# RMSNorm with each row written twice: one 32 KB store run per partition, one DMA queue, fused multiply

## The chip, the cores and the metric

The kernel runs on one core of one Trainium2 chip. The metric is device microseconds (us) per execution, as the median of several runs; lower is better. Single runs that were over 1.5% above the fastest of the same kernel are called slow and are left out of the ratios.

## The reference

```python
x: (8, 512, 2048) float32, gamma: (2048,) float32
x_rep = np.repeat(x, 2, axis=1)                       # every row twice, next to each other
rms = np.sqrt((x_rep ** 2).mean(axis=-1, keepdims=True) + 1e-6)
return x_rep / rms * gamma                            # (8, 1024, 2048) float32
```

At least 33.56 MB must be read from HBM and 67.11 MB written to it.

## The kernel before

A tile is 128 partitions x 2 rows x 2048 elements (16 KB per partition, 2 MB); there are 16 tiles. Loads go out on SP's hardware DMA queue, stores on GpSimd's software queue, two stores per tile, one for each copy of the rows.

```python
K = 2
x_t   = x_f.rearrange("(n p k) d -> n p k d", p=P, k=K)
out_t = out_v.rearrange("(n p k) r d -> n p k r d", p=P, k=K)
BUFS = 6                                   # 6 input tiles, 6 work/output tiles
# ... gamma is loaded first, on SP, and broadcast to all partitions by GpSimd ...
for i in range(ntiles):
    x_tile = xin.tile([P, K, D], f32)
    nc.sync.dma_start(out=x_tile[:], in_=x_t[i])
    sq_tile = sq.tile([P, K, D], f32)
    for k in range(K):                     # ACT: squares and their sum
        nc.scalar.activation(out=sq_tile[:, k, :], in_=x_tile[:, k, :], func=Square,
                             accum_out=ss[:, k : k + 1])
    # ... ACT: rms = sqrt(ss / D + eps); DVE: rstd = 1 / rms ...
    y_tile = sq_tile                       # the squares' tile is used again for the output
    for k in range(K):
        nc.vector.tensor_scalar_mul(out=y_tile[:, k, :], in0=x_tile[:, k, :], scalar1=rstd[:, k : k + 1])
    nc.vector.tensor_mul(out=y_tile[:], in0=y_tile[:], in1=gamma_kd)
    for r in range(R):                     # two stores; HBM runs of one row, 8 KB
        nc.gpsimd.dma_start(out=out_t[i, :, :, r, :], in_=y_tile[:])
# ... (cut)
```

## Time and profile before

| | before |
|---|---|
| time, median | 245.0 us |
| span of the profiled run | 243.0 us |
| DVE / ACT busy | 46% / 29% |
| HBM read, written | 33.56 MB, 67.11 MB |

The page of the kernel before, its utilisation rows (40 equal slices of the span of 6.1 us; a digit is the busy share in tenths, the last row is GB/s of all 16 DMA engines) and its DMA queues (packets, MB, share of the time of 16 engines):

```profile
DVE  0069999950900049680095709577595600000000
...
DMA  6999999999999999999999999999999999999993
GB/s 222 431 431 431 391 433 429 436 417 442 422 431 430 433 422 431 429 427 430 425 430 450 410 426 426 430 425 430 429 425 418 418 417 419 430 417 425 417 426 160
...
q0 software_dynamic: 8704, 67.11, 65.7%
q1 hardware_dynamic: 2306, 33.56, 32.8%
```

The DMA row is full from the second slice to the last but one. No engine comes near it, so the time is the time that the DMA engines need. The costliest groups of instructions (line, engine, operation, operands, count; then busy us, mean ns of one; then the engine's idle time before them and who ended it):

```profile
L64 ACT ACTIVATE sq_tile<-x_tile 128x2048 f32<-128x2048 f32 x32 | 60.8, 1901 | 114.1 <-DMA out_dram<-sq_tile 101.1
L87 DVE TENSOR_TENSOR sq_tile<-sq_tile,gamma_b 128x4096 f32<-128x4096 f32 x16 | 70.8, 4422 | 0.5
...
L84 DVE TENSOR_SCALAR sq_tile<-x_tile,rstd 128x2048 f32<-128x2048 f32 x32 | 40.2, 1298 | 0.5
```

ACT's 101 us of waiting for a store to leave is a buffer coming free late: a sign of the DMA bound, not a cost. The trace also has a record of every DMA packet. A load is 2048 packets of 16 KB, nearly all of 611 ns; the stores are 8192 packets of 8 KB, nearly all of 309 ns.

### The profile page before, as it was taken

The page shows a single profiled execution, that of the slowest core. Times are in us where ns is not written, and L with a number is a line of the kernel's source. Part 1 is how long each engine was busy: PE and PEld are TensorE (multiplying, and loading weights), DVE is VectorE, ACT ScalarE, POOL GpSimd, SP SyncE. Part 2 cuts the span into 40 slices and gives each one's busy share as a digit, 9 for nine tenths or more (in the row PEclk, how much of TensorE's full clock was granted, in tenths as well). Part 3 has the DMA queues.
Part 4 walks back from the last instruction along what each step waited for, and adds up shares of the span by engine and source line. Part 5 has one row for each costly group of instructions (what it writes and reads, how often), then busy time and mean ns, then how long its engine had stood idle before and what let it go on. Part 6 is the DMA issues. An engine that isn't in the chain of part 4 may idle for free.

```text
span 243.0 us, 320 instructions
## 1 busy us (share of the span) xinstructions
DVE 112.7 (46%) x65; ACT 69.5 (29%) x82; POOL 30.2 (12%) x37
## 2 busy tenths in 40 slices
DVE  0069999950900049680095709577595600000000
ACT  2598656006000150600615061541624000000000
POOL 4003223411010101110130111111121111000000
DMA  6999999999999999999999999999999999999993
GB/s 222 431 431 431 391 433 429 436 417 442 422 431 430 433 422 431 429 427 430 425 430 450 410 426 426 430 425 430 429 425 418 418 417 419 430 417 425 417 426 160
DMA packets 11012, 100.69 MB, mean 414 GB/s; under 512 B 769, under 2 KB 769, under 8 KB 769
## 3 DMA queue, kind: packets, MB, share of 16 engines
q0 software_dynamic: 8704, 67.11, 65.7%
q1 hardware_dynamic: 2306, 33.56, 32.8%
q14 instruction: 2, 0.02, 0.0%
HBM read 33.56 MB, written 67.11 MB: 414 GB/s over the span
## 4 chain that ended last, share of the span: by engine, by line
DMA 50%; another core or an unknown queue 15%; issue 4%; ACT 3%; DVE 2%; POOL 1%; POOLq 0%; ACTq 0%
DMA out_dram<-sq_tile 50%; ACT sq_tile L64 3%; DVE sq_tile L87 2%; POOL out_dram L90 1%; POOLq L116 0%; ACT rms L72 0%; DVE rstd L80 0%; ACTq L64 0%; POOLq L90 0%
## 5 line engine op out<-in xcount | busy, mean ns | idle before, releaser
L64 ACT ACTIVATE sq_tile<-x_tile 128x2048 f32<-128x2048 f32 x32 | 60.8, 1901 | 114.1 <-DMA out_dram<-sq_tile 101.1
L87 DVE TENSOR_TENSOR sq_tile<-sq_tile,gamma_b 128x4096 f32<-128x4096 f32 x16 | 70.8, 4422 | 0.5
L90 POOL DMA_DIRECT2D out_dram<-sq_tile x32 | 27.7, 867 | 169.3 <-DMA out_dram<-sq_tile 125.6
L84 DVE TENSOR_SCALAR sq_tile<-x_tile,rstd 128x2048 f32<-128x2048 f32 x32 | 40.2, 1298 | 0.5
L80 DVE RECIPROCAL rstd<-rms 128x2 f32<-128x2 f32 x16 | 2.6, 163 | 77.8 <-ACT rms L72 77.8
L64 ACT ACTIVATION_READ_ACCUMULATOR sq_tile<-x_tile 128x1 f32 x32 | 6.0, 186 | 0.0
L72 ACT ACTIVATE rms<-ss,eps_t 128x2 f32<-128x2 f32 x16 | 4.7, 296 | 0.5
L45 POOL PARTITION_BROADCAST gamma_b<-gamma_b x1 | 2.3, 2293 | 2.1 <-DMA gamma_b<-in_gamma_dram 2.1
L64 ACT ACT_TABLE_LOAD x1 | 1.3, 1283 | 0.7 <-PEq L105 0.7
L72 ACT ACT_TABLE_LOAD x1 | 1.3, 1283 | 0.0
L53 DVE MEMSET eps_t<- 128x1 f32 x1 | 0.1, 59 | 0.8 <-PEq L105 0.8
L105 POOL MEMSET const-float32-0.0<- 128x1 f32 x1 | 0.1, 99 | 0.2 <-issue 0.2
L105 POOL MEMSET const-uint8-127<- 128x1 uint8 x1 | 0.1, 103 | 0.0
L105 POOL MEMSET const-bfloat16-1.0<- 128x1 bf16 x1 | 0.1, 102 | 0.0
L105 POOL MEMSET const-float32-1.0<- 128x1 f32 x1 | 0.1, 99 | 0.0
## 6 DMA issues: line engine op xcount, KB each, us to landing
out_dram<-sq_tile POOLq DMA_DIRECT2D x32, 2048.0 KB, 40.7
x_tile<-in_x_dram SPq DMA_DIRECT2D x16, 2048.0 KB, 24.4
gamma_b<-in_gamma_dram SPq DMA_DIRECT2D x1, 8.0 KB
```

The costliest lines, as they stand in the source:

```text
L45: nc.gpsimd.partition_broadcast(out_ap=gamma_b[:], in_ap=gamma_b[0:1, :])
L53: nc.vector.memset(eps_t, eps)
L64: nc.scalar.activation(out=sq_tile[:, k, :], in_=x_tile[:, k, :], func=mybir.ActivationFunctionType.Square, accum_out=ss[:, k : k + 1],)
L72: nc.scalar.activation(out=rms[:], in_=ss[:], func=mybir.ActivationFunctionType.Sqrt, scale=inv_d, bias=eps_t[:],)
L80: nc.vector.reciprocal(out=rstd[:], in_=rms[:])
L84: nc.vector.tensor_scalar_mul(out=y_tile[:, k, :], in0=x_tile[:, k, :], scalar1=rstd[:, k : k + 1])
L87: nc.vector.tensor_mul(out=y_tile[:], in0=y_tile[:], in1=gamma_kd)
L90: nc.gpsimd.dma_start(out=out_t[i, :, :, r, :], in_=y_tile[:])
L105: nc = _bacc.Bacc("TRN2", target_bir_lowering=False, num_devices=1)
```

## The change

The intent: fewer and longer DMA runs. The output buffer holds both copies of a row, so a tile goes out as one DMA with one 32 KB run per partition, on SP's hardware queue behind the loads. DVE multiplies by the reciprocal and by gamma in one pass and copies the result; the squares go to PSUM, where nobody reads them. There are five input and three output buffers, and the first load is issued before gamma's.

```diff
-    BUFS = 6
-    xin = ctx.enter_context(tc.tile_pool(name="xin", bufs=BUFS))
-    sq = ctx.enter_context(tc.tile_pool(name="sq", bufs=BUFS))
+    AHEAD = 5
+    xin = ctx.enter_context(tc.tile_pool(name="xin", bufs=AHEAD))
+    yout = ctx.enter_context(tc.tile_pool(name="yout", bufs=3))
+    junk = ctx.enter_context(tc.tile_pool(name="junk", bufs=1, space=bass.MemoryType.PSUM))
 ...
+    out_t = out.rearrange("b s d -> (b s) d").rearrange("(n p j) d -> n p (j d)", p=P, j=K * R)
+    load(0)
+    # ... gamma, now on ACT's queue; then load(1) to load(AHEAD - 1)
     for i in range(ntiles):
-        y_tile = sq_tile
+        y = yout.tile([P, K, R, D], f32, name="y")
 ...
         for k in range(K):
-            nc.vector.tensor_scalar_mul(
-                out=y_tile[:, k, :], in0=x_tile[:, k, :], scalar1=rstd[:, k : k + 1]
-            )
-        nc.vector.tensor_mul(out=y_tile[:], in0=y_tile[:], in1=gamma_kd)
-        for r in range(R):
-            nc.gpsimd.dma_start(out=out_t[i, :, :, r, :], in_=y_tile[:])
+            nc.vector.scalar_tensor_tensor(
+                out=y[:, k, 0, :], in0=xt[:, k, :], scalar=rstd[:, k : k + 1], in1=gamma_b[:],
+                op0=Alu.mult, op1=Alu.mult,
+            )
+            nc.vector.tensor_copy(out=y[:, k, 1, :], in_=y[:, k, 0, :])
+        nc.sync.dma_start(out=out_t[i], in_=y.rearrange("p k r d -> p (k r d)"))
+        if i + AHEAD < ntiles:
+            load(i + AHEAD)
```

(Cut: the squares, square root and reciprocal, which only change buffers.)

More of the change, by code (lines that the diff above doesn't have):

```diff
@@ L19 @@
     P = nc.NUM_PARTITIONS
+    f32 = mybir.dt.float32
+    Act = mybir.ActivationFunctionType
+    Alu = mybir.AluOpType
     B, S, D = x.shape
@@ L23 @@
     R = So // S
-    assert D == Do and B == Bo and So == S * R
+    assert R == 2 and D == Do and B == Bo and So == S * R
     eps = 1e-6
-    x_f = x.rearrange("b s d -> (b s) d")
+    inv_d = 1.0 / float(D)
+    K = 2
     N = B * S
-    K = 2
     assert N % (P * K) == 0
     ntiles = N // (P * K)
-    x_t = x_f.rearrange("(n p k) d -> n p k d", p=P, k=K)
-    out_v = out.rearrange("b (s r) d -> (b s) r d", r=R)
-    out_t = out_v.rearrange("(n p k) r d -> n p k r d", p=P, k=K)
-    BUFS = 6
+    x_t = x.rearrange("b s d -> (b s) d").rearrange("(n p k) d -> n p k d", p=P, k=K)
@@ L41, with load @@
     small = ctx.enter_context(tc.tile_pool(name="small", bufs=8))
-    gamma_b = singles.tile([P, D], mybir.dt.float32)
-    nc.sync.dma_start(out=gamma_b[0:1, :], in_=gamma.partition_broadcast(1))
-    nc.gpsimd.partition_broadcast(out_ap=gamma_b[:], in_ap=gamma_b[0:1, :])
-    gamma_kd = bass.AP(
-        tensor=gamma_b.tensor,
-        offset=gamma_b.offset,
-        ap=[gamma_b.ap[0], [0, K], gamma_b.ap[1]],
-    )
-    eps_t = singles.tile([P, 1], mybir.dt.float32)
+    xs = []
+    def load(i):
+        xt = xin.tile([P, K, D], f32, name="xt")
+        nc.sync.dma_start(out=xt[:], in_=x_t[i])
+        xs.append(xt)
@@ L53 @@
+    load(0)
+    gamma_b = singles.tile([P, D], f32, name="gamma_b")
+    nc.scalar.dma_start(out=gamma_b[0:1, :], in_=gamma.partition_broadcast(1))
+    nc.gpsimd.partition_broadcast(out_ap=gamma_b[:], in_ap=gamma_b[0:1, :])
+    eps_t = singles.tile([P, 1], f32, name="eps_t")
     nc.vector.memset(eps_t, eps)
-    inv_d = 1.0 / float(D)
+    for i in range(1, AHEAD):
+        load(i)
     for i in range(ntiles):
-        x_tile = xin.tile([P, K, D], mybir.dt.float32, name="x_tile")
-        nc.sync.dma_start(out=x_tile[:], in_=x_t[i])
-        sq_tile = sq.tile([P, K, D], mybir.dt.float32, name="sq_tile")
-        ss = small.tile([P, K], mybir.dt.float32, name="ss")
+        xt = xs[i]
+        y = yout.tile([P, K, R, D], f32, name="y")
+        ss = small.tile([P, K], f32, name="ss")
@@ L63 @@
         for k in range(K):
-            nc.scalar.activation(
-                out=sq_tile[:, k, :],
-                in_=x_tile[:, k, :],
-                func=mybir.ActivationFunctionType.Square,
-                accum_out=ss[:, k : k + 1],
-            )
-        rms = small.tile([P, K], mybir.dt.float32, name="rms")
-        nc.scalar.activation(
-            out=rms[:],
-            in_=ss[:],
-            func=mybir.ActivationFunctionType.Sqrt,
-            scale=inv_d,
-            bias=eps_t[:],
-        )
@@ L79 @@
-        rstd = small.tile([P, K], mybir.dt.float32, name="rstd")
-        nc.vector.reciprocal(out=rstd[:], in_=rms[:])
-        y_tile = sq_tile
-        for k in range(K):
-            nc.vector.tensor_scalar_mul(
-                out=y_tile[:, k, :], in0=x_tile[:, k, :], scalar1=rstd[:, k : k + 1]
-            )
-        nc.vector.tensor_mul(out=y_tile[:], in0=y_tile[:], in1=gamma_kd)
-        for r in range(R):
-            nc.gpsimd.dma_start(out=out_t[i, :, :, r, :], in_=y_tile[:])
+            sq = junk.tile([P, D], f32, name="sq")
@@ new lines @@
+            nc.scalar.activation(out=sq[:], in_=xt[:, k, :], func=Act.Square, accum_out=ss[:, k : k + 1])
+        rms = small.tile([P, K], f32, name="rms")
+        nc.scalar.activation(out=rms[:], in_=ss[:], func=Act.Sqrt, scale=inv_d, bias=eps_t[:])
+        rstd = small.tile([P, K], f32, name="rstd")
+        nc.vector.reciprocal(out=rstd[:], in_=rms[:])
+        for k in range(K):
+            nc.vector.scalar_tensor_tensor(
+                out=y[:, k, 0, :], in0=xt[:, k, :], scalar=rstd[:, k : k + 1], in1=gamma_b[:],
+                op0=Alu.mult, op1=Alu.mult,
+            )
+            nc.vector.tensor_copy(out=y[:, k, 1, :], in_=y[:, k, 0, :])
```

## The prediction

> **What bounds it now.** The DMA engines. The utilisation rows show their share at 9 tenths or more in 38 of 40 slices, 414 GB/s mean over the span and about 430 in the middle; DVE is busy 46%. HBM traffic is 33.56 MB read and 67.11 MB written, unchanged. The waits view agrees: ACT waits 101 us and POOL 126 us for stores.
>
> **Packet cost.** In the trace's packet records a load is 2048 packets of 16 KB, nearly all 611 ns; a store is 8192 packets of 8 KB, nearly all 309 ns. Two sizes give an estimate: 302 ns per 8 KB plus about 7 ns per packet. At the floor, loads cost 2048 x 611 / 16 = 78.2 us and stores 8192 x 309 / 16 = 158.2 us, together 236.4 of the 237.7 us between the first and the last data packet. The rest of the 243.0 us span is 2.1 us before the first packet and about 3 us after the last. About 1 us is store packets of 312 to 319 ns; about 1 us is slow first packets of the load stream; and about 0.6 us (estimate) is the dip to 395 GB/s at 24 to 30 us, where load packets stretch as the first store starts. The Trainium skill ("DMA: Bandwidth & Descriptors", section "Bandwidth") gives a 435 GB/s fabric ceiling; these durations give 429 (16 KB) and 424 (8 KB).
>
> **What the change does.**
> - Stores become one 32 KB run per partition on SP's hardware queue. If one packet carries it: 4 x 302 + 7 = 1215 ns (estimate) against 4 x 309 = 1236, which saves 2.7 us over 2048 runs on 16 engines; if cut at 16 KB, 1222 ns and 1.8 us saved. [...]
> - The first load is issued before gamma: about 0.4 us earlier.
> - The software queue goes, perhaps with the dip and slow late packets: 0 to 1.5 us.
> - DVE: the two scale passes and the 4.42 us multiply per tile (7.05 us with the reciprocal) become two fused multiplies (estimate 2.2 us each, half of 4.42) and two copies (estimate 1.3, as the scale pass): about 7.2 us per tile. Hidden under 14.6 us of DMA per tile.
> - Squares go to PSUM: no effect.
> - Three output buffers and one in-order queue of store i, load i+5. A store's buffer comes free, DVE needs 7 us, and two other stores and three loads (about 34 us, estimate) are still queued: the queue should not run dry. The first store is ready near 21.6 us, before the five loads end.
>
> All the gain is DMA packet time, on the critical path; the DVE changes are off it.
>
> **Prediction.** Span: 1.7 to the first packet + 78.2 + 155.5 to 156.4 + about 2 of slow packets + 2.7 = about 240.4 us; plus the 2.0 us by which the time exceeds the span: 242.4 us. Range 240.0 to 244.6. Faster by over 2% (under 240.1): 0.11; within 2%: 0.86; slower: 0.03.
>
> **What would show it.** Store packets of 32 KB near 1215 ns (or 16 KB near 611); no software queue; DMA share 9 everywhere; no dip; mean near 419 GB/s.
>
> **What would make it wrong.** Slow packets vanish entirely or run packets exceed my line: under 240. In-order queueing leaves gaps, or 32 KB stores run at more ns per byte: over 245.

## The result, and the profile after

The changed kernel takes 244.01 us (243.73 to 244.77, four runs) against 245.0 us. The ratio is 0.9964, with a 95% interval of 0.9948 to 0.9981. A ratio here is the mean time of one kernel's fast runs over that of the other's of the same rounds, so it is not quite the ratio of the medians. The time lies within the predicted range, but the change is 1.0 us where 2.6 us were forecast.

The page after:

```profile
DVE  0069986528073370743709238082470915692000
...
DMA  7999999999999999999999999999999999999991
GB/s 253 433 433 428 430 433 417 433 401 460 406 455 433 403 452 409 452 433 422 433 406 436 425 430 433 420 441 422 433 439 422 439 433 433 433 433 433 433 422 49
...
q1 hardware_dynamic: 4608, 100.67, 97.5%
```

```profile
L73 DVE SCALAR_TENSOR_TENSOR y<-xt,rstd,gamma_b 128x2048 f32<-128x2048 f32 x32 | 73.8, 2349 | 63.0 <-DMA out_dram<-y 62.8
L67 ACT ACTIVATE sq<-xt 128x2048 f32<-128x2048 f32 x32 | 60.2, 1880 | 124.1 <-DMA xt<-in_x_dram 123.6
L77 DVE COPY y<-y 128x2048 f32<-128x2048 f32 x32 | 37.7, 1219 | 0.0
```

DVE is about as predicted: 2.35 and 1.22 us per pass (forecast 2.2 and 1.3), 7.3 us per tile with the reciprocal. The rates of the stretch with stores alone rose from 417 to 430 GB/s before to 433 after. Yet the last slice moves only 49 GB/s, with a 1 in the DMA row. The next view cuts the end of both kernels into windows. Columns: window in us, its length, busy time of DVE, ACT and POOL with counts, PE clock, DMA share of 16 engines, GB/s. A packet is counted whole where it begins, so a share can exceed 1, and a window can show 0 while an earlier packet ends in it. First the kernel before:

```profile
237.00:238.00 1.00, 0.00 (x0) 0.00 (x0) 0.00 (x0) 1.00 1.00 418
238.00:239.00 1.00, 0.00 (x0) 0.00 (x0) 0.00 (x0) 1.00 0.87 360
239.00:240.00 1.00, 0.00 (x0) 0.00 (x0) 0.00 (x0) 1.00 0.41 172
240.00:241.00 1.00, 0.00 (x0) 0.00 (x0) 0.00 (x0) 1.00 0.04 16
```

and the changed kernel:

```profile
233.00:235.00 2.00, 0.00 (x0) 0.00 (x0) 0.00 (x0) 1.00 1.10 475
235.00:236.00 1.00, 0.00 (x0) 0.00 (x0) 0.00 (x0) 1.00 0.53 229
236.00:237.00 1.00, 0.00 (x0) 0.00 (x0) 0.00 (x0) 1.00 0.23 98
237.00:238.00 1.00, 0.00 (x0) 0.00 (x0) 0.00 (x0) 1.00 0.15 66
238.00:239.00 1.00, 0.00 (x0) 0.00 (x0) 0.00 (x0) 1.00 0.23 98
239.00:240.00 1.00, 0.00 (x0) 0.00 (x0) 0.00 (x0) 1.00 0.08 33
```

Before, the sixteen engines stop nearly together: their last parts land within 1.8 us. After, most of them are done between 236 and 237 us, and for four more microseconds one to four engines work on alone: a share of 0.08 is one packet of 1.2 us. A DMA of the changed kernel is 128 packets, and following the packets of one engine from end to start in the trace gives eight for each of the 16 engines in every DMA. This share is fixed, so an engine that has fallen behind can hand nothing over.

The trace records when each of the 16 engines lands its part of a DMA. From these records I take, for a DMA, the median engine, the last engine, and their difference, called the lag.

| last store | median engine | last engine | lag | span | last landing to end |
|---|---|---|---|---|---|
| before | 239.76 | 240.89 | 1.1 | 243.03 | 2.14 |
| changed | 236.56 | 241.12 | 4.6 | 242.06 | 0.94 |

This is the account of the result. The median engine is 3.2 us earlier (and the mean of the sixteen is 2.4 us earlier, 237.43 against 239.78): the predicted gain is there. The last engine is 0.2 us later: the lag has eaten all of it. The 1.0 us that is left comes from the end of the program, where 1.2 us were saved. There, before, GpSimd's drain is the wait that ends last. Instructions of the closing line in the kernel before (count, then ns minimum/median/maximum, first and last start):

```profile
L116 SPq EVENT_SEMAPHORE  x11: 17/28/28, 240.9 to 243.0; - x11
...
L116 POOLq DRAIN  x3: 46/108/41055, 201.2 to 242.8; - x3
```

and in the changed one:

```profile
L106 SPq EVENT_SEMAPHORE  x7: 17/28/21527, 219.5 to 242.0; - x7
...
L106 POOLq DRAIN  x3: 34/83/2416, 2.3 to 241.8; - x3
```

The drain of 41.06 us began at 201.19 and ended at 242.24, 1.35 us after the last landing; with no software queue in use there is none to wait for. SP's waits are a second, smaller part: after the last landing it steps through nine of them before and two after, about 0.06 us each. Before, SP was through at 241.53 us, 0.7 us ahead of the drain's end, so about 0.7 of the 1.2 us is the drain and the rest the shorter row of waits. before_fused and run8k_pool, which also store 8 KB runs by the software queue, show the same drain, 1.36 us after the last landing; no run without stores on that queue does.

How the lag comes about is in the same records. It grows at the loads and hardly shrinks again. The lag in the changed kernel at some of its loads, by the time at which the median engine landed the load:

| us | 28 | 57 | 86 | 115 | 130 | 145 | 159 | 188 | last store |
|---|---|---|---|---|---|---|---|---|---|
| lag | 0.5 | 1.0 | 2.1 | 2.4 | 3.6 | 3.7 | 4.2 | 4.5 | 4.6 |

The 2048 store packets are all 1213 to 1228 ns, but 51 load packets after 32 us are stretched by over 40 ns, up to 762 ns: 15.0 us in sum over all engines. They are not spread evenly. Of the load packets that end while nine or more other engines are storing, 23% are stretched; of the others, 1.1%. In two later traces of this kernel it is 20% against 1.3%, and 16% against 1.0%. (A stretched packet ends later, which by itself could put it among the first group. Counted instead at 611 ns after each packet's start, the shares are 21% against 1.4%, 19% against 1.5% and 14% against 1.4%, so this is not the reason.) So it is mostly the engine that is behind, still loading when the others have gone on to store, that loses more. In the kernel before, the load packets after 32 us are stretched by 0.7 us in sum.

### The profile page after: what moved, and what is told of

Same layout as the page of the kernel before. It is cut to its first block, busy times and chain, and to the rows that moved or that the text cites. A ratio compares the mean times of both kernels' runs of the same rounds, so it can differ in the third digit from the quotient of the medians.

```text
span 242.1 us, 296 instructions
## 1 busy us (share of the span) xinstructions
DVE 112.5 (46%) x81; ACT 71.2 (29%) x82; POOL 2.5 (1%) x5
## 4 chain that ended last, share of the span: by engine, by line
DMA 70%; DVE 16%; ACT 2%; issue 1%; DVEq 1%
DMA out_dram<-y 67%; DVE y L73 11%; DVE y L77 5%; DMA xt<-in_x_dram 3%; ACT sq L67 1%; ACT L69 1%; DVEq L106 0%; ACT rms L69 0%; DVE rstd L71 0%; DVEq L73 0%
## 5 line engine op out<-in xcount | busy, mean ns | idle before, releaser
L73 DVE SCALAR_TENSOR_TENSOR y<-xt,rstd,gamma_b 128x2048 f32<-128x2048 f32 x32 | 73.8, 2349 | 63.0 <-DMA out_dram<-y 62.8
L67 ACT ACTIVATE sq<-xt 128x2048 f32<-128x2048 f32 x32 | 60.2, 1880 | 124.1 <-DMA xt<-in_x_dram 123.6
L77 DVE COPY y<-y 128x2048 f32<-128x2048 f32 x32 | 37.7, 1219 | 0.0
L67 ACT ACTIVATION_READ_ACCUMULATOR sq<-xt 128x1 f32 x32 | 6.0, 186 | 0.0
```

The costliest lines, as they stand in the source:

```text
L67: nc.scalar.activation(out=sq[:], in_=xt[:, k, :], func=Act.Square, accum_out=ss[:, k : k + 1])
L73: nc.vector.scalar_tensor_tensor(out=y[:, k, 0, :], in0=xt[:, k, :], scalar=rstd[:, k : k + 1], in1=gamma_b[:], op0=Alu.mult, op1=Alu.mult,)
L77: nc.vector.tensor_copy(out=y[:, k, 1, :], in_=y[:, k, 0, :])
```

## The experiments

The table gives all runs; stretch is packet time over 611 ns (16 KB), 309 ns (8 KB) or 1213 ns (32 KB) after 32 us, summed over all engines. The kernel before had a median of 244.97 to 245.02 us. A profile is of one run, the time of all. The traced run is the slowest of its set in store_act, store_pool, run8k_pool and after_side, and the second slowest in after_again, so the lags of these rows are probably larger than those of a run at the median.

| run | time | ratio to before | median engine | lag | stretch of loads / stores |
|---|---|---|---|---|---|
| before | 245.0 | 1 | 239.76 | 1.1 | 0.7 / 17.1 |
| changed | 244.01 | 0.9964 | 236.56 | 4.6 | 15.0 / 0.3 |
| after_again | 243.80 | 0.9971 | 236.50 | 6.2 | 21.0 / 0.4 |
| after_side | 243.65 | 0.9950 | 236.49 | 6.2 | 12.7 / 0.6 |
| group2_sp | 242.70 | 0.9901 | 236.57 | 3.3 | 5.4 / 0.8 |
| group4_sp | 240.69 | 0.9823 | 236.56 | 1.3 | 4.0 / 0.5 |
| group4_side | 241.24 | 0.9851 | 236.53 | 2.0 | 5.1 / 0.7 |
| half_mix | 243.38 | 0.9933 | 237.86 | 2.3 | 3.7 / 1.0 |
| load8_sp | 242.99 | 0.9916 | 238.04 | 2.3 | 13.1 / 1.5 |
| run8k_sp | 250.49 | 1.0223 | 238.88 | 9.4 | 24.4 / 4.4 |
| run8k_pool | 246.25 | 1.0030 | 239.57 | 3.4 | 15.3 / 12.3 |
| store_act (slow run) | 246.38 | 0.9928 | 240.22 | 6.8 | 1.9 / 71.2 |
| store_pool | 246.52 | 1.0053 | 245.74 | 0.1 | 27.2 / 20.3 |
| load_pool16 | 244.09 | 0.9967 | 239.89 | 0.9 | 7.7 / 23.3 |
| no_reload | 186.29 | - | 182.98 | 0.5 | - / 0.8 |
| before_fused | 246.66 | 1.0060 | 240.47 | 1.3 | 6.1 / 23.4 |
| align2_sp | 267.99 | - | 265.17 | 0.1 | 20.6 / 85.1 |
| group2x_sp | 243.37 | 0.9938 | 239.63 | 1.1 | 33.3 / 19.3 |

My first theory D was that the lag belongs to one in-order queue. Its rivals: R, the 32 KB runs as such; F, certain engines are always slow.

### The changed kernel again, and two queues

**after_again** (no edit)

> The changed kernel once more, for a second trace and as the base for the three others. Theory D (drift): in one in-order queue the sixteen DMA engines change from loads to stores nearly together; the load packets of an engine that is behind are stretched when the others begin to store, so it falls further behind, and nothing in the program evens the engines out. D expects again 15 to 30 us of load packet time above 611 ns in sum over all engines, most of it after 32 us, and the last engine ending 2 to 5 us after the median engine; which engines lag is left to chance. Theory R (runs): the 32 KB store packets hold off loads on all engines, whatever the queue; it expects the same here. Theory F (fixed): certain engines are always slow; same here too. Time 243.5 to 244.8.

Measured: 243.80 us, 243.34 to 246.11 in six runs, a wider spread than the 0.6 us of the kernel before. The profiled run, of 245.49 us, has a lag of 6.2 us with the median engine again at 236.50. The lag is there again, with another size, beyond the 2 to 5 us that D expected. The interval of the ratio, 0.9939 to 1.0003, just includes no gain at all over the kernel before.

**store_act**

```diff
-        nc.sync.dma_start(out=out_t[i], in_=y...)
+        # on ACT's queue, after the squares of the next tile
+        nc.scalar.dma_start(out=out_t[i - 1], in_=ys[i - 1]...)
```

> The changed kernel with the stores on ACT's hardware queue and the loads alone on SP's, so that each DMA engine takes packets of both in turn; 32 KB runs and buffers as they were. D: excess of load packets after 32 us falls under 3 us in sum, engines end within 2 us of each other as in the kernel before, last data packet at 237 to 239 us, time 240.5 to 242.5, faster than the changed kernel by about 1%. R: stretched loads remain, time 243.5 to 245. F: the last engine stays 3 to 5 us behind, time as the changed kernel.

Measured: six runs from 241.32 to 249.71 us, three of them slow, and the profile fell on a slow one. There the loads are hardly stretched, as D said, but now the stores are, by 71 us in sum, and the lag is 6.8 us. The engines fell into two groups of eight, landing at 236.7 to 237.2 and 243.3 to 247.0 us, so the median of the table lies between the groups. As only a slow run was profiled, this can't explain the fast ones (241.32, 244.12 and 244.41). Inconclusive.

**store_pool**

```diff
-        nc.sync.dma_start(out=out_t[i], in_=y...)
+        nc.gpsimd.dma_start(out=out_t[i], in_=y...)
```

> As store_act, but the stores on GpSimd's software queue, as in the kernel before. D: engines even, last data packet at 237 to 239 us as with ACT. The end of the program after the last data packet was 2.5 us in the kernel before and 1.3 us in the changed one; if that belongs to the software queue it is 2.5 us here, and the time is 1 to 1.3 us above store_act: 241.5 to 243.5. R and F: 244.5 to 246.

Measured: 246.52 us, slower than before, which missed D's forecast, for a reason I had not thought of. In the traced run, the slowest of seven (249.07 us; the others took 245.95 to 247.14), the engines ran dry. Windows of this run:

```profile
110.00:114.00 4.00, 0.12 (x2) 3.79 (x5) 0.00 (x0) 1.00 0.92 393
114.00:118.00 4.00, 4.00 (x3) 0.00 (x0) 0.00 (x0) 1.00 0.28 115
118.00:122.00 4.00, 2.85 (x3) 2.55 (x3) 0.53 (x1) 1.00 0.68 188
122.00:126.00 4.00, 2.18 (x2) 1.75 (x3) 0.00 (x0) 1.00 1.04 373
```

The Trainium skill ("DMA: Bandwidth & Descriptors", section "Queues, rings and completion order") says that an engine takes packets of its queues in turn, whole packets at a time. The trace agrees: from 30 to 40 us there are 92 store packets of 32 KB and 77 load packets of 16 KB. In load_pool16 below, with equal packets, it is 131 to 132. So here the loads get a little under a third of the bytes, no more than they need and no lead. In addition DVE computes the reciprocal of the next tile before it multiplies this one, so a store can wait for the next load. Before the gap the lag of a DMA had grown to 5.0 us, so two queues alone did not prevent it; that the engines end within 0.2 us of each other is no evidence: the lag fell to 0.8 us after this gap, grew to 2.6 us again, and fell to 0.1 us after a second gap (204 to 206 us, DMA share 0.12), so it is the gaps that let all start anew. At the restart, 119 to 126 us, 53 load packets are stretched by 26.5 us: again loads that meet the first stores. The other forecast, an end of 2.5 us after the last data packet, failed as well: it was 1.8 us here, and the drain ended 0.7 us after the last landing.

**run8k_sp**

```diff
-        nc.sync.dma_start(out=out_t[i], in_=y...)
+        for r in range(R):                                  # 8 KB runs, one queue
+            nc.sync.dma_start(out=out_r[i, :, :, r, :], in_=y[:, :, r, :])
```

> The changed kernel with each store cut into two DMAs of 8 KB runs (one for each copy of the rows), still on SP's one queue: only the packet size goes back. D: stretched loads and drift stay (10 to 30 us of excess in sum after 32 us, last engine 2 to 5 us after the median), store packets 309 ns again, about 2 us more DMA per engine: time 245.5 to 247, slower than before. R: stretched loads vanish, engines even, time 243.5 to 244.5.

Measured: 250.49 us, ratio 1.0223, lag 9.4 us, loads stretched by 24.4 us in sum. R falls: with the store packets back at 309 ns the lag is larger than ever. D's sign was right, its size too small.

### The number of changes between loads and stores

**group2_sp**

```diff
-        if i + AHEAD < ntiles:
-            load(i + AHEAD)
+        if i % 2 == 1:                                      # store, store, load, load
+            for j in (i - 1, i):
+                if j + AHEAD < ntiles:
+                    load(j + AHEAD)
```

> The changed kernel with stores and loads in groups of two on the one SP queue (two stores, two loads): half as many changes between stores and loads, same packets. Theory D (load packets of a lagging engine are stretched when the others begin to store): stretch after 32 us falls to about half of the changed kernel's 15 to 20 us in sum, last engine 1 to 3 us after the median, time 242 to 243.5. Rival S (stretch comes of the mix of reads and writes as such, so it follows the bytes loaded, not the changes): as the changed kernel, 243.3 to 244.5.

Measured: 242.70 us, ratio 0.9901; lag 3.3 us; stretch of loads 5.4 us. The median engine is at 236.57, where it was in the changed kernel. Same packets and same queue in another order give back over 1 us more. The time is as D forecast; the lag is a little over its 1 to 3 us, the stretch less than the half that it named.

**half_mix**

```diff
+        for k in range(K):                                  # half a tile out, half a tile in
+            nc.sync.dma_start(out=out_k[i, :, k], in_=y[:, k]...)       # 16 KB runs
+            nc.sync.dma_start(out=xs[j][:, k], in_=x_t[j, :, k])        # 8 KB runs
```

> The other way: store half a tile (16 KB runs), load half a tile (8 KB runs), twice as many changes on the one SP queue. Packets cost about 1.4 us more per engine (from steps of 306, 608 and 1210 ns for 8, 16 and 32 KB). D: 20 to 40 us of stretch in sum, last engine 4 to 8 us after the median, time 246 to 249. S: stretch as before, time 245 to 246.

Measured: 243.38 us, lag 2.3 us, stretch 3.7 us. Both forecasts are wrong. Twice as many changes did not double the lag, so their number is not all that counts. The bursts and the load packets are half as long here, and this run can't say which of these it is.

**no_reload**

```diff
-            load(i + AHEAD)
+            xs.append(xs[i])                                # only five tiles are ever loaded
```

> Wrong result on purpose: only the first five tiles are loaded, all sixteen stores follow, so only one change from loads to stores. D and S: no stretch after 32 us, engines end within 0.8 us of each other, though stores are as in the changed kernel; if certain engines are slow by themselves (F), the last still ends 2 us or more late. Span about 5 x 4.87 + 16 x 9.68 + 5 = 184 us, time about 186.

Measured: 186.29 us; the last store lands from 182.56 to 183.49 us on the sixteen engines, lag 0.5 us. F falls: sixteen 32 KB stores in a row leave no engine behind. The lag needs loads among the stores. The records carry no engine number, so whether it is the same engines that fall behind in the one-queue runs is not shown.

**load_pool16**

```diff
-        nc.sync.dma_start(out=xt[:], in_=x_t[i])
+        nc.gpsimd.dma_start(out=xt[:], in_=x_t[i])
 ...
-        nc.sync.dma_start(out=out_t[i], in_=y...)
+        for k in range(K):                                  # 16 KB runs
+            nc.sync.dma_start(out=out_k[i, :, k], in_=y[:, k]...)
```

> Loads on GpSimd's software queue, stores on SP's in two DMAs of 16 KB runs. store_pool starved because each engine takes packets of the two queues in turn, and with 32 KB against 16 KB the loads get only the third of the bytes that they need, with no lead; equal packets give the loads half, so they run ahead and no engine should run dry. D: no stretch but at the first stores, engines end within 1.5 us of each other, last data packet at 238 to 239.5 us, DMA share 9 in every slice, time 241 to 243.5. If two queues lose by themselves, whatever the sizes: time over 244.5.

Measured: 244.09 us. The queues share as forecast (from 40 to 50 us 131 load and 132 store packets), nothing runs dry and the lag is 0.9 us at the end; but packets are stretched by 31 us in sum, mostly stores, the median engine is at 239.89, and the time is over D's 241 to 243.5. Two queues spread the loss over all engines here; they don't remove it. D's claim that the stretch belongs to the one queue falls.

### Fewer returns, smaller packets, and two controls

From here on D says only: a return from loads to stores costs an engine that is behind more than the others.

**group4_sp**

```diff
-        if i + AHEAD < ntiles:
-            load(i + AHEAD)
+        for j in {3: (5, 6, 7, 8), 7: (9, 10, 11, 12), 10: (13, 14, 15)}.get(i, ()):
+            load(j)
```

> As group2_sp, but the reloads come in three groups (four, four and three tiles, after stores 3, 7 and 10) on the one SP queue: three returns from loads to stores instead of eleven, same packets. So far the last engine's last store landed 4.6 and 6.2 us after the median engine in the changed kernel (11 returns) and 3.3 us in group2_sp (6 returns), the median at about 236.5 us in all three. Theory D (each return lets lagging engines lose more): last minus median 1 to 2.3 us, time 241.0 to 242.2, faster than both kernels. If the number of returns is not what counts (half_mix had twice as many and a lag of only 2.3): lag over 3 us, time over 242.6.

Measured: 240.69 us, ratio 0.9823 (0.9806 to 0.9841), the best of all and a little under D's 241.0 to 242.2. The median engine is at 236.56, exactly as in the changed kernel; the lag is 1.3 instead of 4.6 us. The spans differ by 242.06 - 238.79 = 3.27 us and the lags by 4.56 - 1.28 = 3.28 us. Its rows and the windows of its end:

```profile
DMA  7999999999999999999999999999999999999994
GB/s 254 423 428 434 401 434 439 439 439 439 439 401 434 434 467 423 417 428 428 434 434 434 423 428 464 434 439 423 409 425 434 434 439 439 439 439 434 439 423 203
```

```profile
235.00:236.00 1.00, 0.00 (x0) 0.00 (x0) 0.00 (x0) 1.00 0.53 229
236.00:237.00 1.00, 0.00 (x0) 0.00 (x0) 0.00 (x0) 1.00 0.08 33
237.00:238.00 1.00, 0.00 (x0) 0.00 (x0) 0.00 (x0) 1.00 0.00 0
```

From 235 to 236 us it is as in the changed kernel (0.53); then a single packet begins where the changed kernel went on until 240. The gain that the prediction promised is here.

**load8_sp**

```diff
-        nc.sync.dma_start(out=xt[:], in_=x_t[i])
+        for k in range(K):                                  # 8 KB runs
+            nc.sync.dma_start(out=xt[:, k], in_=x_t[i, :, k])
```

> The changed kernel with each load cut in two DMAs of 8 KB runs; stores of 32 KB, order and number of returns as in the changed kernel. half_mix had short bursts and small load packets together; this has the small packets alone. Theory P (it is the 16 KB load packets that get stretched): stretch of loads after 32 us under 6 us in sum, lag of the last engine under 2.5 us, time 242.0 to 243.2. Theory B (it is the length of the bursts of loads and stores): lag 4 us or more as in the changed kernel, time 243.8 to 245.5.

Measured: 242.99 us, lag 2.3 us, stretch 13.1 us. Neither theory as stated: the lag is P's, the stretch nearly B's. Smaller load packets bring a smaller lag, at the price of a median engine 1.5 us later.

**run8k_pool** (run8k_sp with its stores on GpSimd's queue)

```diff
-            nc.sync.dma_start(out=out_r[i, :, :, r, :], in_=y[:, :, r, :])
+            nc.gpsimd.dma_start(out=out_r[i, :, :, r, :], in_=y[:, :, r, :])
```

> run8k_sp with one word changed: the 8 KB stores go out on GpSimd's software queue, so queues and packets are those of the kernel before, while buffers, fused multiply, PSUM squares and gamma are those of the changed kernel. If the lag of 9.4 us in run8k_sp comes of the one queue: lag under 1.5 us, stretch of loads after 32 us under 5 us, time 244.3 to 245.6, like the kernel before. If it comes of the new buffers: lag over 4 us, time over 248.

Measured: 246.25 us (245.01 to 247.28), lag 3.4 us. Changing only the queue took the lag from 9.4 to 3.4 us and the time down by 4.2 us, so the one queue does carry most of it with these packets. But it did not come down to the 1.1 us of the kernel before, so the rest of the change (buffers, order, fused multiply) may have its part. This is not shown: the traced run is the slowest of four, two of which (245.01 and 245.37) are about as fast as the kernel before, and the interval of the ratio, 0.9994 to 1.0066, includes 1.

**before_fused** (the kernel before, with the fused multiply alone)

```diff
-            nc.vector.tensor_scalar_mul(out=y_tile[:, k, :], in0=x_tile[:, k, :], scalar1=rstd[:, k : k + 1])
-        nc.vector.tensor_mul(out=y_tile[:], in0=y_tile[:], in1=gamma_kd)
+            nc.vector.scalar_tensor_tensor(out=y_tile[:, k, :], in0=x_tile[:, k, :],
+                scalar=rstd[:, k : k + 1], in1=gamma_b[:], op0=mult, op1=mult)
```

> The kernel before with the fused multiply alone (two 2.35 us passes a tile for two 1.24 us and one 4.42 us). All theories: DVE busy falls from 113 to about 78 us and the time stays at 244.7 to 245.3.

Measured: DVE falls to 76.3 us, and the time rises to 246.66 us, ratio 1.0060 (1.0040 to 1.0080). An engine that is idle half the time got faster and the kernel slower. In the trace the packets are stretched more (loads 6.1 us in sum against 0.7, stores 23.4 against 17.1), and the median engine is 0.7 us later. So DVE is not quite off the path. My reading is that it sets when stores start, and with that what meets what in the DMA engines; that is not shown, and which meeting costs it I can't say.

**align2_sp** (group2_sp, with stores held until the loads before them have landed)

```diff
+        for src in (xs[-1], xt):        # adds 0 * the last loaded element to one output column
+            nc.vector.scalar_tensor_tensor(out=y[:, 1, 1, 0:1], in0=src[:, K - 1, D - 1 : D],
+                scalar=0.0, in1=y[:, 1, 1, 0:1], op0=Alu.mult, op1=Alu.add)
```

> group2_sp with two one-column operations per tile that add zero times the last loaded element to the output: each pair of stores now waits until the last load queued before it has landed from all engines, at the price of an idle gap of some 2 to 3 us at each of seven returns (time about 255 to 265, not the point). Theory D (a load packet is stretched when other engines begin to store): the stretched loads at 24 to 28 us, present in every run so far with 5 to 10 us in sum, and those after 32 us (5.4 us in group2_sp) both vanish: under 1.5 us in sum after 20 us; the last engine stays within 0.7 us of the median throughout. If the loads stretch by themselves: 8 us or more in sum after 20 us.

Measured, in one run, whose state is unknown: 267.99 us, over the forecast of 255 to 265. At the first change from loads to stores, where group2_sp stretches its loads by 7.5 us in sum between 20 and 32 us, it is 0.0. That part of D holds: no store begun elsewhere, no stretched load. The lag stays at 0.8 us or less. But stretched loads (20.6 us) and stores (85.1 us) appear at the other change, when loads follow stores without a wait and all engines change at once. So the forecast of under 1.5 us in all was wrong: either change can stretch packets. D is at best half of the mechanism.

**group2x_sp**

```diff
-    AHEAD = 5                                               # and yout bufs=3
+    AHEAD = 7                                               # and yout bufs=2
 ...
+        for j in {4: (7, 8, 9, 10, 11), 8: (12, 13, 14, 15)}.get(i, ()):
+            load(j)
```

> Seven input buffers and two output buffers, reloads in two groups (five and four tiles, after stores 4 and 8): two returns after the first, same packets, same SBUF. D: last engine 0.5 to 1.4 us after the median, time 240.0 to 241.0. The risk is the second output buffer missing: if the stores run dry between tiles, DMA share falls under 9 in the middle slices and the time is over 242.

Measured: 243.37 us. The lag is small (1.1 us), as forecast, but the stretch is far larger than in group4_sp (33.3 us of loads and 19.3 us of stores against 4.0 and 0.5), spread over all engines, and the median engine is 3 us later (239.63). One change at 107 to 111 us takes 14 us of it. The risk that I had named is not the reason: by the packet records the engines ran dry only at 130 us, for 0.3 us. Fewer returns are not better without limit, or the third output buffer matters; what differs at these changes stays open.

**after_side and group4_side** (no edit; one chip, same rounds)

> The changed kernel a third time, next to group4_side on one chip. If the account holds: median engine's last store at 236.4 to 236.7 us again, the last engine 3 to 7 us later, time 243.3 to 245.

> group4_sp a second time. If the account holds: median engine at 236.4 to 236.7 us as in the changed kernel, the last engine 0.8 to 2.3 us later, time 240.2 to 241.6, so 2.5 to 4 us below after_side. If its small lag was luck: lag over 3 us, time over 242.5.

Measured: 243.65 us with a lag of 6.2 us, against 241.24 us with a lag of 2.0 us; the median engines at 236.49 and 236.53. The ratio of the two is 241.37 / 244.14 = 0.989 (means of the fast runs). Both lags are there again. The medians lie 2.4 us apart, a little under the forecast of 2.5 to 4. The trace of after_side is of its slowest run (245.46 us), that of group4_side of a run at the median. A run of after_side at the median has a span of 241.8 us; with the same median engine and the same 0.94 us at the end, its lag would be about 4.4 us (estimate: 241.8 - 0.94 - 236.49).

## Why the prediction was right or wrong

- **DMA bound, same bytes: right.** The DMA row is full in both kernels.
- **Packets of 32 KB near 1215 ns: right.** They take 1213 ns. Summed and divided by 16, packet time fell from 238.9 to 235.8 us (stores 4.0 us less, loads 0.9 us more), and the median engine's last landing came 3.2 us earlier.
- **First load 0.4 us earlier: right.** The first load packet starts at 1.73 instead of 2.10 us.
- **"The software queue goes, perhaps with the dip and slow late packets": half.** The slow late store packets (17.1 us of stretch in sum before) went. The stretched loads at the first stores stayed: 7.5 us in sum before, 7.8 after, between 20 and 32 us.
- **"The queue should not run dry": right** for the changed kernel; SP's waits for DVE never emptied it.
- **The step that failed** is "All the gain is DMA packet time, on the critical path", and in the sum the use of the term "about 2 of slow packets". I added up packet time over all engines and divided by 16. That sum came out: 78.2 + 155.5 to 156.4 + 2 is 235.7 to 236.6 us, and 235.8 were measured. But the slow packets are not shared out evenly, the kernel ends with its slowest engine, and each engine's share of the work is fixed. By the sum the last data packet was due at about 237.7 us (240.4 - 2.7); it ended at 240.78, 3.1 us later. The last engine came 4.6 us after the median (6.2 us in two more traces), where the kernel before had 1.1 us. That took 3.4 us, more than the whole gain of the median engine. The prediction named gaps and slower stores as dangers, not unequal engines. It had a hint in hand: it gives 237.7 us between the first and the last data packet of the kernel before, but the trace has 2.10 to 240.57, which is 238.5 us, so there too the last packet ended later than the sum of 236.4 us says.
- **A second term was mis-sized:** the 2.7 us after the last data packet. It measured 242.06 - 240.78 = 1.3 us, mostly because GpSimd's drain no longer ends last. The 1.0 us gained is this term, which I had left nearly unchanged (it was 243.03 - 240.57 = 2.5 us before). So two errors partly cancel: the last packet was forecast 3.1 us too early and the end after it 1.4 us too long. That the time lies within the range is in part luck.
- **"The DVE changes are off it": not shown, and doubtful.** The fused multiply alone made the kernel before 0.6% slower.

Shown: where the gain went (the lag), that it builds up at the loads of a one-queue order, and that grouping the reloads brings it out, at 240.69 and 241.24 us. Shown too, at the first change and in one run: loads are not stretched if no engine begins to store while they run. Open: why packets are stretched when loads and stores change over, why 8 KB load packets leave less lag, why group2x_sp loses so much at its changes, and whether it is always the same engines that lag.

## What to carry to other kernels

In a DMA-bound kernel, predict the slowest DMA engine, not the mean: look at the last slices of the DMA row for a tail in which a few engines work alone. When loads and stores share one in-order queue, try issuing them in groups, so that they change over less often; here three groups of reloads in place of eleven single ones were worth 1.1 to 1.4% with the same bytes and packets. But measure it, since two still larger groups, with one output buffer less, lost most of it again.

## What the Trainium skill lacked or had wrong

- "DMA: Bandwidth & Descriptors", sections "Issuing engines are not separate DMA queues" and "Rules for kernel authors": they say that issuing from several engines only saves the time to issue. Here moving 8 KB stores from SP's to GpSimd's queue, with nothing else changed, took the time from 250.49 to 246.25 us and the lag of the last engine from 9.4 to 3.4 us (the runs were on two chips, with the kernel before at 244.98 and 245.02 us; the queue is then also a software one, so this does not tell a second queue from another kind of queue).
- The same page says nothing of engines falling behind one another when loads and stores change over: a lag of 4.6 to 6.2 us of 242 us with eleven returns on one queue, 1.3 to 2.0 us with three, and load packets of 611 ns stretched, after 32 us, to as much as 1373, 1876 and 1780 ns in the three traces of the changed kernel.
- The same page, section "Queues, rings and completion order", has engines take turns by packets of about 9 to 17 descriptors. In these traces a packet record is one run of 8, 16 or 32 KB (309, 611, 1213 ns), and on one engine the runs of two queues alternate one by one, so the run length sets each queue's share: 92 store packets of 32 KB against 77 load packets of 16 KB in 10 us.
- No page that I read has the cost of the software queue at a program's end: GpSimd's drain ended 1.35 us after the last landing of the kernel before, and 0.7 us after it in store_pool, which has half as many DMAs on that queue.
